# Layer norm and partial sums between attention and the feed-forward stage of a one-core encoder layer: where sums, scales and quarter sums are computed and in which order

## The chip, the core and the metric

The kernel runs on one core of a Trainium2 chip. The metric is the device time of one launch in microseconds (us), the median of several runs. Engines are named as in the profile: PE (matrix products), DVE, ACT and POOL (element-wise work), SP (which here only issues transfers).

## The reference

One transformer-like layer over 1056 tokens (1024 prompt tokens and 32 of a running stream) of width 1024. What matters here is the part after the mixers, with `x` the residual stream and `mix` the concatenated convolution and attention outputs times `w_o`:

```python
x = _layernorm(ALPHA * x + mix, ln1_g, ln1_b)     # mean, centred square mean, rsqrt, times g plus b
hid = relu(x @ w_ff1)                             # 1024 -> 4096
ff = (hid * hid) @ w_ff2                          # 4096 -> 1024
x = _layernorm(ALPHA * x + ff, ln2_g, ln2_b)
```

## The kernel before, in words

All activations stand transposed: features on the 128 partitions, tokens along the free axis. The 1024 features are eight row tiles, held in pairs: `z[i]` is 128 x 2 x 1056 in float32, and tile j is `z[j // 2][:, j % 2]`. Products are made to float32 precision from three half products: each operand is split into a rounded part `hi` and a rest `lo` (`split`, lines 106 to 111: `hi` on ACT in line 108, `lo` by a subtraction in line 111 on POOL or DVE), and `dense` (lines 127 to 133) issues hi*hi, hi*lo and lo*hi for each row tile k, in that order, on PE.

Tokens are cut three ways. CHUNKS are three blocks of 384, 384 and 288 tokens for the output projection and the first layer norm (chunk 0 is the last to be done). QUARTERS are four blocks of 264 tokens, counted from the end, so that quarter 3 and most of quarter 2 lie in or touch chunk 0. Halves of 528 tokens, together with halves of the features, give four blocks "11", "12", "21", "22", from which the fast matrix product of the feed-forward stage (seven products in place of eight) forms sums "t1" to "t4".

Between attention and feed-forward stands a list of short jobs, MID (lines 53 to 54), worked through in order (lines 832 to 834) by `job` (lines 692 to 713). A job's name is a kind, a chunk or quarter number and an index:
- `w0d`: output projection of attention for tile d of chunk 0 (`w_o_attn`, line 640 adds the product from PSUM to z on DVE).
- `lc0`, `lc1`, `lc2`: layer norm of chunk c: `ln_mean` (line 649: three DVE or POOL additions of tile pairs into one, line 652: PE products with a matrix of 1/1024, which leave the mean on every partition), `ln_var` (line 660: subtract the mean on DVE; lines 662 and 665: squares on ACT; line 666: three additions; line 669: PE products), `ln_scale` (line 674: square root on ACT; line 675: reciprocal on DVE; line 678: eight DVE instructions, z times g times 1/sigma). Chunk 2 adds on POOL, chunks 1 and 0 on DVE.
- `xc0`: `x1_out`: for each of the eight tiles ACT writes `hi` of z + b (line 784) and z + b itself (line 785), DVE (odd tiles) or POOL (even tiles) the rest `lo` (line 788); then z goes to memory in four transfers (line 790) on SP's queue.
- `fqe`: quarter q of four feature blocks e (CLASSIC) that are done by the ordinary product: 24 PE products of 264 columns, then a relu on ACT (line 798) and a product on DVE (line 799), which frees the PSUM bank, and a transfer out. Quarters 0 and 1 need chunks 2 and 1; quarters 2 and 3 need chunk 0, after `x00`.
- `tt`: `combine_x1` (lines 804 to 830): eight 1056-column subtractions on DVE (lines 823, 825, 826, 828) for the quarter sums, and eight splits of them (`split_sum`, lines 815 to 818: `hi` on ACT, `lo` on DVE or POOL). "t4" takes the place of block "12", which the jobs `f0e` and `f1e` read.

PSUM banks of this stage come from a pool of six ("mm2", lines 731 and 760) and one for the norms ("st_b", line 507). In this part a planner (the tile framework's simulated schedule) puts the instructions in order: the program's order is the priority, and the planner's cost estimates decide which instruction is put into an engine's queue next. On the chip each queue then runs strictly in that order.

After MID comes the feed-forward loop (`ff1_steps`, lines 870 to 953) in an order written out by hand: steps of 24 PE products (lines 856 to 858) with `run` (lines 1144 to 1157), which issues each step's loads and weight splits some steps ahead. The first seven steps use blocks 11, 21, t2, t1, t3, 22, t4 in that order; the second step adds onto the PSUM bank of the first, which ACT must have read before (line 906).

Of the kernel before, what the change touches and what calls it, by code (L numbers as in the profile page):

```python
# [15 lines left out]
OP = mybir.AluOpType  # L16
# [33 lines left out]
    (1, ("w13", "w14", "", "")),  # L50
    (0, ("", "w15", "w16", "w17")),
)
MID = tuple("w00 w01 w02 x20 w03 w04 l10 l11 l12 x10 w05 w06 w07 l00 f00 f10 f01 l01 f11 l02 x00 tt "
            "f20 f30 f21 f31 f02 f12 f22 f32 f03 f13 f23 f33".split())


def native(t, g2, i0):
# [12 lines left out]
def hybrid_layer(ctx, tc, xT, win, wkw, wo, w1, w2, ckT, cv, ckiT, scT, cw, lnp, rb, cst, oh,  # L70
# [574 lines left out]
    def ln_mean(c0, n, add_eng):  # L645
# [6 lines left out]
            PE.matmul(mean[:, :n], ones, s1[:, a], start=(a == 0), stop=(a == 1))  # L652
        return mean

    def ln_var(c0, n, add_eng, mean):
        cols = slice(c0, c0 + n)
        s2 = wide("junka", n)
        for i in range(4):
            zi = z[i][:, :, cols]
            V.tensor_tensor(zi, zi, mean[:, None, :n].to_broadcast([128, 2, n]), op=OP.subtract)  # L660
            if i == 0:
                S.activation(s2, zi, AF.Square)
            else:
                sq = wide("tie" if i % 2 else "rank", n)
                S.activation(sq, zi, AF.Square)
                add_eng.tensor_tensor(s2, s2, sq, op=OP.add)
        var = st_ps()
        for a in range(2):
            PE.matmul(var[:, :n], ones, s2[:, a], start=(a == 0), stop=(a == 1))
        return var  # L670

    def ln_scale(c0, n, which, var):
        rstd = scr.tile([128, 384], F32, name="rstd")
        S.activation(rstd[:, :n], var[:, :n], AF.Sqrt, bias=eps)
        V.reciprocal(rstd[:, :n], rstd[:, :n])
        for j in range(8):
            zj = z[j // 2][:, j % 2, c0:c0 + n]
            V.scalar_tensor_tensor(zj, zj, lnw[:, 2 * which, j:j + 1], rstd[:, :n], op0=OP.mult, op1=OP.mult)

    def ln(c0, n, which, add_eng):  # L680

        mean = ln_mean(c0, n, add_eng)
        ln_scale(c0, n, which, ln_var(c0, n, add_eng, mean))

    def conv_job(d):
        w = load_w(wo[d][:, 0:512], 4, 128)
# [5 lines left out]
    def job(name):  # L692
        if name == "tt":
            return combine_x1()
        kind, c, d = name[0], int(name[1]), int(name[2])
        if kind == "c":
            conv_job(d)
        elif kind == "w":
            w_o_attn(d, *CHUNKS[c], w=w_first[d] if c == 0 and d < 3 else None)
        elif kind == "t":  # L700
            topk((d,), True)
        elif kind == "x":
            x1_out(*CHUNKS[c])
        elif kind == "f":
            if d not in first:
                first[d] = load_w(w1[CLASSIC[d]], 8, 128)
            ff1(d, first[d], QUARTERS[c])
        elif d == 0:
            st[c] = ln_mean(*CHUNKS[c], (G if c == 2 else V))
        elif d == 1:  # L710
            st[c] = ln_var(*CHUNKS[c], (G if c == 2 else V), st[c])
        else:
            ln_scale(*CHUNKS[c], 0, st[c])

    for t, jobs in PLAN:
        for g2 in range(4):
# [61 lines left out]
    def x1_out(c0, n):  # L778
        cut = min(max(H - c0, 0), n)
        for j in range(8):  # L780
            zj, b = z[j // 2][:, j % 2, c0:c0 + n], lnw[:, 1, j:j + 1]
            spans = [(o, w) for o, w in ((0, cut), (cut, n - cut)) if w]
            for o, w in spans:
                S.activation(x1_part(j, c0 + o, w)[0], zj[:, o:o + w], AF.Identity, bias=b)
            S.activation(zj, zj, AF.Identity, bias=b)
            for o, w in spans:
                hi, lo = x1_part(j, c0 + o, w)
                (V if j % 2 else G).tensor_tensor(lo, zj[:, o:o + w], f32(hi), op=OP.subtract)
        for i in range(4):
            nc.sync.dma_start(zd[2 * i:2 * i + 2, :, c0:c0 + n].rearrange("j p t -> p j t"), z[i][:, :, c0:c0 + n])  # L790
# [13 lines left out]
    def combine_x1():  # L804
# [10 lines left out]
        def split_sum(name, i, raw, eng):  # L815
            hi = xf[name][:, 0, 2 * i:2 * i + 2]
            S.activation(hi, raw, AF.Copy)
            eng.tensor_tensor(xf[name][:, 1, 2 * i:2 * i + 2], raw, f32(hi), op=OP.subtract)

        for i in range(2):  # L820
            b11, b12 = z[i][:, :, :H], z[i][:, :, H:]
            b21, b22 = z[2 + i][:, :, :H], z[2 + i][:, :, H:]
            V.tensor_tensor(b11, b12, b11, op=OP.subtract)
            split_sum("t1", i, b11, V)
            V.tensor_tensor(b12, b22, b12, op=OP.subtract)
            V.tensor_tensor(b22, b22, b11, op=OP.subtract)
            split_sum("t2", i, b22, V)
            V.tensor_tensor(b21, b21, b22, op=OP.subtract)
            split_sum("t3", i, b12, G)
            split_sum("t4", i, b21, G)  # L830

    first = {}
    for name in MID:
# [310 lines left out]
    def run(steps, ahead, ahead_load):  # L1144

        n, prepared = len(steps), 0
        for i in range(-ahead_load, n):
            if i + ahead_load < n:
                for f in steps[i + ahead_load].load:
                    f()  # L1150
            while prepared < min(n, i + ahead + 1 if i > 0 else min(2, i + ahead + 1)):
                for f in steps[prepared].prep:
                    f()
                prepared += 1
            if i >= 0:
                for f in steps[i].mm + steps[i].post:
                    f()
# [293 lines left out]
```

## Time and profile before

| | us |
|---|---|
| median of 3 runs | 1326.07 (1323.88 to 1326.92) |
| the profiled execution, its own time | 1326.95 |
| its span, first to last instruction | 1325.2 |
| PE busy in the span | 1237.5 (93%) |
| DVE, ACT, POOL busy | 976.5, 692.7, 565.5 |

PE is nearly always busy; what can be gained is where it is not, or where its granted clock is low. "Busy" of PE is the union of pipelined instructions whose ends are modelled, so the pitch from start to start is the better price of one product. Times in the rows are us from the start of the span unless marked ns.

### The profile page before, as it was taken

What the parts mean: (1) busy time and instruction counts of PE and PEld (TensorE: products, weight loads), DVE (VectorE), ACT (ScalarE), POOL (GpSimd) and SP (SyncE); (2) the same over time, 40 slices, a digit from 0 to 9 for tenths busy, and PEclk for the clock granted to TensorE, in tenths of its full rate; (3) what the DMA queues carried; (4) which work ended last, traced back from release to release, by engine and by line L of the source; (5) the groups of instructions that cost most, each with busy time, mean ns of one, the idle gap of its engine ahead of it and who ended that gap; (6) DMA issues with size and microseconds to landing.
All of it is one profiled execution on the core that took longest, in us unless ns stands there. A gap on an engine that the chain in (4) does not pass through costs nothing. (4 is left out here: it accounts for less than half of the span.)

```text
span 1325.2 us, 24062 instructions
## 1 busy us (share of the span) xinstructions
PE 1237.5 (93%) x8822; PEld 1199.8 (91%) x8822; DVE 976.5 (74%) x2023; ACT 692.7 (52%) x1378; POOL 565.5 (43%) x452
## 2 busy tenths in 40 slices
PE   7999999998899989787899999999999999998894
PEld 6999999988898978676899999999999999998884
DVE  5675899999478888698466766767567567587766
ACT  5666988743798897765322222222434444443323
POOL 2412444523521342363444355444444444447632
PEclk9999999998999998897999999999999999999987
DMA  6321111135621221242134444344953653642201
GB/s 205 98 71 37 33 49 48 49 122 165 165 68 27 57 64 34 64 160 99 60 121 154 155 138 154 127 150 157 336 190 97 212 180 107 186 139 81 66 34 66
DMA packets 97221, 149.98 MB, mean 113 GB/s; under 512 B 12456, under 2 KB 41808, under 8 KB 97104
## 3 DMA queue, kind: packets, MB, share of 16 engines
q1 hardware_dynamic: 81664, 139.55, 32.4%
q0 software_dynamic: 9504, 4.33, 1.9%
q10 hardware_dynamic: 5936, 4.58, 1.2%
q8 instruction: 69, 1.13, 0.4%
q14 instruction: 48, 0.39, 0.1%
HBM read 105.41 MB, written 43.00 MB: 112 GB/s over the span
## 5 line engine op out<-in xcount | busy, mean ns | idle before, releaser
L111 POOL TENSOR_TENSOR whl<-wraw,whl 128x512 fp32r<-128x512 f32 (+1 forms) x184 | 251.7, 1373 | 413.1 <-ACT whl L108 394.1
L856 PE MATMUL acc<-b,whl 128*128 128x264 f32 x1088 | 310.9, 286 | 5.8 <-DVE ring L935 2.7
L857 PE MATMUL acc<-b,whl 128*128 128x264 f32 x1088 | 310.7, 286 | 0.0
L858 PE MATMUL acc<-b,whl 128*128 128x264 f32 x1088 | 309.2, 284 | 0.0
L856 PEld LDWEIGHTS acc<-b,whl 128*128 128x128 f32 x1088 | 205.5, 189 | 6.8 <-DVE ring L935 2.9
L108 ACT ACTIVATE whl<-wraw 128x512 fp32r<-128x512 f32 (+1 forms) x184 | 113.2, 623 | 178.8 <-DVE wraw L851 152.2
L858 PEld LDWEIGHTS acc<-b,whl 128*128 128x128 f32 x1088 | 206.0, 189 | 0.0
L857 PEld LDWEIGHTS acc<-b,whl 128*128 128x128 f32 x1088 | 205.1, 188 | 0.1
L132 PE MATMUL mm<-area,whl 128*128 128x384 f32 (+4 forms) x552 | 180.6, 328 | 0.4 <-DVE area L111 0.4
L131 PE MATMUL mm<-xh,whl 128*128 128x384 f32 (+4 forms) x520 | 170.2, 329 | 9.7 <-ACT whl L108 5.5
L133 PE MATMUL mm<-xh,whl 128*128 128x384 f32 (+4 forms) x520 | 169.0, 329 | 0.5 <-POOL whl L111 0.5
L111 DVE TENSOR_TENSOR b<-xraw,b 128x528 fp32r<-128x528 f32 x94 | 69.8, 742 | 86.4 <-ACT b L108 86.2
L108 ACT ACTIVATE b<-xraw 128x528 fp32r<-128x528 f32 x94 | 60.5, 644 | 135.5 <-PE acc L858 79.9
L441 ACT ACTIVATE junka<-s,cand 128x1024 bf16<-128x1024 f32 (+1 forms) x93 | 96.3, 1036 | 31.3 <-DVE cand L454 25.9
L131 PEld LDWEIGHTS mm<-xh,whl 128*128 128x128 f32 (+1 forms) x520 | 97.0, 187 | 12.5 <-ACT whl L108 6.2
L132 PEld LDWEIGHTS mm<-area,whl 128*128 128x128 f32 (+1 forms) x552 | 103.3, 187 | 3.2 <-DVE area L111 1.2
L133 PEld LDWEIGHTS mm<-xh,whl 128*128 128x128 f32 (+1 forms) x520 | 96.8, 187 | 4.0 <-POOL whl L111 1.4
L111 POOL TENSOR_TENSOR whl<-at,whl 128x512 fp32r<-128x512 f32 x56 | 81.0, 1457 | 30.7 <-ACT whl L108 30.7
L443 DVE TENSOR_SCALAR_CACHE_REDUCE junk<-s,cand 128x384 bf16<-128x384 f32 (+1 forms) x124 | 80.2, 647 | 1.1
L856 PE MATMUL acc<-area,whl 128*128 128x264 f32 x240 | 69.0, 287 | 0.0
L858 PE MATMUL acc<-area,whl 128*128 128x264 f32 x240 | 68.7, 286 | 0.0
L857 PE MATMUL acc<-area,whl 128*128 128x264 f32 x240 | 68.6, 286 | 0.0
(309 smaller groups left out, 3326.0 us busy)
## 6 DMA issues: line engine op xcount, KB each, us to landing
hd<-ring SPq DMA_DIRECT2D x98, 264.0 KB, 2.1
xraw<-hd SPq DMA_DIRECT2D x98, 264.0 KB, 2.7
at<-in_w_dram SPq DMA_DIRECT2D x58, 256.0 KB, 3.6
wraw<-in_win_dram SPq DMA_DIRECT2D x52, 256.0 KB, 2.6
wraw<-in_wo_dram SPq DMA_DIRECT2D x40, 256.0 KB, 2.7
w_a<-in_w_dram SPq DMA_DIRECT2D x23, 256.0 KB, 3.7
w_c<-in_w_dram SPq DMA_DIRECT2D x19, 256.0 KB, 3.2
zz<-zd SPq DMA_DIRECT2D x4, 1056.0 KB, 8.0
```

The costliest lines, as they stand in the source:

```text
L108: S.activation(hi, raw, AF.Copy)
L111: (lo_eng or G).tensor_tensor(lo, raw, f32(hi), op=OP.subtract)
L131: PE.matmul(ps, wh[k], a, start=(k == 0), stop=False)
L132: PE.matmul(ps, wh[k], b, start=False, stop=False)
L133: PE.matmul(ps, wl[k], a, start=False, stop=(k == K - 1))
L441: S.activation(junk(R, N), s, AF.Sign, bias=c, scale=-1.0, accum_out=cnt[:R, i:i + 1])
L443: V.tensor_scalar(junk(R, N), s, c, -float(k), op0=OP.is_ge, op1=OP.add, accum_out=cnt[:R, i:i + 1])
L856: PE.matmul(ps, wh, xhi, start=start, stop=False, skip_group_check=more)
L857: PE.matmul(ps, wh, xlo, start=False, stop=False, skip_group_check=more)
L858: PE.matmul(ps, wl, xhi, start=False, stop=stop, skip_group_check=more)
```

## The change

- Mean of chunk 0: the three additions and two PE products go; in their place PE multiplies each of the eight row tiles by the 1/1024 matrix, tile d - 1 after projection job d, all into one bank of the pool of six (`total`). Job `l00` then does nothing.
- Variance of chunk 0: the three additions go; each square goes into PE products by itself, eight in all (`ln_var_pe`). Chunks 1 and 2 keep their additions.
- Scale, all chunks: four DVE products of a tile pair with 1/sigma in place of eight with g and 1/sigma. g moves into `x1_out`, as the scale operand of the ACT instructions. For chunk 0 the float32 z is written by DVE (times g, plus b) and no longer by ACT.
- Quarter sums: the same eight subtractions and eight splits in the order t2, t1, t3, t4; both `lo` of t1 go from DVE to POOL, one each of t3 and t4 from POOL to DVE.
- MID: `f02` and `f12` come before `x00`, and `f03`, `f13` before `f22`.
- `run`: the preparation of the first feed-forward steps is no longer held to two.

```diff
--- before.py
+++ after.py
@@ -50,8 +50,8 @@
     (1, ("w13", "w14", "", "")),
     (0, ("", "w15", "w16", "w17")),
 )
-MID = tuple("w00 w01 w02 x20 w03 w04 l10 l11 l12 x10 w05 w06 w07 l00 f00 f10 f01 l01 f11 l02 x00 tt "
-            "f20 f30 f21 f31 f02 f12 f22 f32 f03 f13 f23 f33".split())
+MID = tuple("w00 w01 w02 x20 w03 w04 l10 l11 l12 x10 w05 w06 w07 l00 f00 f10 f01 l01 f11 f02 l02 f12 x00 tt "
+            "f20 f30 f21 f31 f03 f13 f22 f32 f23 f33".split())
 
 
 def native(t, g2, i0):
@@ -652,35 +652,42 @@
             PE.matmul(mean[:, :n], ones, s1[:, a], start=(a == 0), stop=(a == 1))
         return mean
 
+    def centred(c0, n, i, mean):
+
+        zi = z[i][:, :, c0:c0 + n]
+        V.tensor_tensor(zi, zi, mean[:, None, :n].to_broadcast([128, 2, n]), op=OP.subtract)
+        sq = wide(("junka", "tie", "rank", "tie")[i], n)
+        S.activation(sq, zi, AF.Square)
+        return sq
+
     def ln_var(c0, n, add_eng, mean):
-        cols = slice(c0, c0 + n)
-        s2 = wide("junka", n)
-        for i in range(4):
-            zi = z[i][:, :, cols]
-            V.tensor_tensor(zi, zi, mean[:, None, :n].to_broadcast([128, 2, n]), op=OP.subtract)
-            if i == 0:
-                S.activation(s2, zi, AF.Square)
-            else:
-                sq = wide("tie" if i % 2 else "rank", n)
-                S.activation(sq, zi, AF.Square)
-                add_eng.tensor_tensor(s2, s2, sq, op=OP.add)
+        s2 = centred(c0, n, 0, mean)
+        for i in range(1, 4):
+            add_eng.tensor_tensor(s2, s2, centred(c0, n, i, mean), op=OP.add)
         var = st_ps()
         for a in range(2):
             PE.matmul(var[:, :n], ones, s2[:, a], start=(a == 0), stop=(a == 1))
         return var
 
-    def ln_scale(c0, n, which, var):
+    def total(ps, d, a):
+
+        PE.matmul(ps, ones, a, start=(d == 0), stop=(d == 7))
+
+    def ln_var_pe(c0, n, mean):
+        var = st_ps()
+        for i in range(4):
+            sq = centred(c0, n, i, mean)
+            for a in range(2):
+                total(var[:, :n], 2 * i + a, sq[:, a])
+        return var
+
+    def ln_scale(c0, n, var):
         rstd = scr.tile([128, 384], F32, name="rstd")
         S.activation(rstd[:, :n], var[:, :n], AF.Sqrt, bias=eps)
         V.reciprocal(rstd[:, :n], rstd[:, :n])
-        for j in range(8):
-            zj = z[j // 2][:, j % 2, c0:c0 + n]
-            V.scalar_tensor_tensor(zj, zj, lnw[:, 2 * which, j:j + 1], rstd[:, :n], op0=OP.mult, op1=OP.mult)
-
-    def ln(c0, n, which, add_eng):
-
-        mean = ln_mean(c0, n, add_eng)
-        ln_scale(c0, n, which, ln_var(c0, n, add_eng, mean))
+        for i in range(4):
+            zi = z[i][:, :, c0:c0 + n]
+            V.tensor_tensor(zi, zi, rstd[:, None, :n].to_broadcast([128, 2, n]), op=OP.mult)
 
     def conv_job(d):
         w = load_w(wo[d][:, 0:512], 4, 128)
@@ -697,6 +704,11 @@
             conv_job(d)
         elif kind == "w":
             w_o_attn(d, *CHUNKS[c], w=w_first[d] if c == 0 and d < 3 else None)
+            if c == 0:
+                if d == 0:
+                    st[0] = mm_ps()
+                for e in ((d - 1, 7) if d == 7 else (d - 1,) if d else ()):
+                    total(st[0][:, :CHUNKS[0][1]], e, z[e // 2][:, e % 2, :CHUNKS[0][1]])
         elif kind == "t":
             topk((d,), True)
         elif kind == "x":
@@ -706,11 +718,12 @@
                 first[d] = load_w(w1[CLASSIC[d]], 8, 128)
             ff1(d, first[d], QUARTERS[c])
         elif d == 0:
-            st[c] = ln_mean(*CHUNKS[c], (G if c == 2 else V))
+            if c:
+                st[c] = ln_mean(*CHUNKS[c], (G if c == 2 else V))
         elif d == 1:
-            st[c] = ln_var(*CHUNKS[c], (G if c == 2 else V), st[c])
+            st[c] = ln_var(*CHUNKS[c], (G if c == 2 else V), st[c]) if c else ln_var_pe(*CHUNKS[0], st[0])
         else:
-            ln_scale(*CHUNKS[c], 0, st[c])
+            ln_scale(*CHUNKS[c], st[c])
 
     for t, jobs in PLAN:
         for g2 in range(4):
@@ -778,11 +791,14 @@
     def x1_out(c0, n):
         cut = min(max(H - c0, 0), n)
         for j in range(8):
-            zj, b = z[j // 2][:, j % 2, c0:c0 + n], lnw[:, 1, j:j + 1]
+            zj, g, b = z[j // 2][:, j % 2, c0:c0 + n], lnw[:, 0, j:j + 1], lnw[:, 1, j:j + 1]
             spans = [(o, w) for o, w in ((0, cut), (cut, n - cut)) if w]
             for o, w in spans:
-                S.activation(x1_part(j, c0 + o, w)[0], zj[:, o:o + w], AF.Identity, bias=b)
-            S.activation(zj, zj, AF.Identity, bias=b)
+                S.activation(x1_part(j, c0 + o, w)[0], zj[:, o:o + w], AF.Identity, scale=g, bias=b)
+            if c0:
+                S.activation(zj, zj, AF.Identity, scale=g, bias=b)
+            else:
+                V.tensor_scalar(zj, zj, g, b, op0=OP.mult, op1=OP.add)
             for o, w in spans:
                 hi, lo = x1_part(j, c0 + o, w)
                 (V if j % 2 else G).tensor_tensor(lo, zj[:, o:o + w], f32(hi), op=OP.subtract)
@@ -817,17 +833,20 @@
             S.activation(hi, raw, AF.Copy)
             eng.tensor_tensor(xf[name][:, 1, 2 * i:2 * i + 2], raw, f32(hi), op=OP.subtract)
 
+        b11, b12 = [z[i][:, :, :H] for i in range(2)], [z[i][:, :, H:] for i in range(2)]
+        b21, b22 = [z[2 + i][:, :, :H] for i in range(2)], [z[2 + i][:, :, H:] for i in range(2)]
         for i in range(2):
-            b11, b12 = z[i][:, :, :H], z[i][:, :, H:]
-            b21, b22 = z[2 + i][:, :, :H], z[2 + i][:, :, H:]
-            V.tensor_tensor(b11, b12, b11, op=OP.subtract)
-            split_sum("t1", i, b11, V)
-            V.tensor_tensor(b12, b22, b12, op=OP.subtract)
-            V.tensor_tensor(b22, b22, b11, op=OP.subtract)
-            split_sum("t2", i, b22, V)
-            V.tensor_tensor(b21, b21, b22, op=OP.subtract)
-            split_sum("t3", i, b12, G)
-            split_sum("t4", i, b21, G)
+            V.tensor_tensor(b11[i], b12[i], b11[i], op=OP.subtract)
+            V.tensor_tensor(b12[i], b22[i], b12[i], op=OP.subtract)
+            V.tensor_tensor(b22[i], b22[i], b11[i], op=OP.subtract)
+            split_sum("t2", i, b22[i], V)
+        for i in range(2):
+            split_sum("t1", i, b11[i], G)
+        for i in range(2):
+            split_sum("t3", i, b12[i], V if i else G)
+        for i in range(2):
+            V.tensor_tensor(b21[i], b21[i], b22[i], op=OP.subtract)
+            split_sum("t4", i, b21[i], V if i else G)
 
     first = {}
     for name in MID:
@@ -1148,7 +1167,7 @@
             if i + ahead_load < n:
                 for f in steps[i + ahead_load].load:
                     f()
-            while prepared < min(n, i + ahead + 1 if i > 0 else min(2, i + ahead + 1)):
+            while prepared < min(n, i + ahead + 1):
                 for f in steps[prepared].prep:
                     f()
                 prepared += 1
```

## Rows read from the trace of the kernel before

**Rows 1.** Windows, all engines: busy us (instructions), PE clock, DMA share, GB/s.
```profile
558.00:576.00 18.00, 18.00 (x102) 17.70 (x102) 12.79 (x14) 14.59 (x32) 12.63 (x12) 0.97 0.50 154
...
593.60:598.00 4.40, 0.07 (x2) 0.07 (x1) 4.22 (x7) 2.15 (x5) 0.00 (x0) 0.86 0.22 76
598.00:605.40 7.40, 2.86 (x4) 1.11 (x4) 3.85 (x4) 1.23 (x3) 0.00 (x0) 0.50 0.03 9
605.40:610.40 5.00, 4.98 (x22) 4.98 (x23) 5.00 (x7) 5.00 (x11) 2.25 (x2) 0.50 0.24 84
610.40:619.80 9.40, 9.40 (x78) 9.24 (x76) 8.65 (x7) 5.18 (x9) 5.93 (x4) 1.00 0.79 264
...
624.10:633.20 9.10, 6.44 (x42) 6.23 (x40) 9.10 (x8) 5.62 (x11) 6.97 (x4) 0.81 0.00 0
```

**Rows 2.** PE timeline, 584 to 653: start, duration, instruction, [idle before <-releaser].
```profile
584.28 1.56 PE L652 MATMUL st_b<-junk,cs 128*128 128x384 f32 x4
...
585.38 0.58 PE L131 MATMUL mm<-b,whl 128*128 128x264 f32 x1
...
597.96 2.90 PE L669 MATMUL st_b<-junka,cs 128*128 128x384 f32 x4 [4.33 <-DVE junka L666]
...
605.42 1.47 PE L131 MATMUL mm<-b,whl 128*128 128x264 f32 x5 [4.56 <-ACT b L784]
...
623.12 0.39 PE L132 MATMUL mm<-b,whl 128*128 128x264 f32 x1 [3.27 <-DVE b L788]
...
633.17 0.39 PE L131 MATMUL mm<-b,whl 128*128 128x264 f32 x1 [2.66 <-DVE xraw L799]
...
652.31 0.29 PE L856 MATMUL acc<-b,whl 128*128 128x264 f32 x1
```

**Rows 3.** DVE timeline, 579 to 640, same columns.
```profile
579.63 1.45 DVE L649 TENSOR_TENSOR junk<-z,z 128x768 f32<-128x768 f32 x1
...
581.94 2.29 DVE L649 TENSOR_TENSOR junk<-junk,z 128x768 f32<-128x768 f32 x2
...
584.15 6.25 DVE L788 TENSOR_TENSOR b<-z,b 128x144 fp32r<-128x144 f32 x6
...
590.66 3.53 DVE L660 TENSOR_TENSOR z<-z,st_b 128x768 f32<-128x768 f32 x4
...
601.51 2.55 DVE L675 RECIPROCAL rstd<-rstd 128x384 f32<-128x384 f32 x1 [3.70 <-ACT rstd L674]
...
604.10 5.08 DVE L678 SCALAR_TENSOR_TENSOR z<-z,lnw,rstd 128x384 f32<-128x384 f32 x8
...
620.28 2.32 DVE L818 TENSOR_TENSOR area<-z,area 128x1056 fp32r<-128x1056 f32 x1
...
622.52 0.55 DVE L788 TENSOR_TENSOR b<-z,b 128x384 fp32r<-128x384 f32 x1
...
638.91 1.25 DVE L818 TENSOR_TENSOR area<-z,area 128x1056 fp32r<-128x1056 f32 x1
```

**Rows 4.** Groups of DVE by line, 470 to 660: count | busy us, mean ns.
```profile
L678 DVE SCALAR_TENSOR_TENSOR z<-z,lnw,rstd 128x384 f32<-128x384 f32 x16 | 12.2, 828 | 0.0
...
L666 DVE TENSOR_TENSOR junka<-junka,tie 128x768 f32<-128x768 f32 x4 | 3.8, 946 | 0.0
```

**Rows 5.** Waits, 557 to 600: engine, line, released by: total us, times, longest.
```profile
PE mm L132 <- DVE b L788: 2.8, 4, 1.2
```

**Rows 6.** Groups of DVE by line, 360 to 420, same columns as rows 4.
```profile
L491 DVE TENSOR_SCALAR s<-s,cand 128x384 f32<-128x384 f32 x2 | 0.8, 404 | 0.0
```

**Rows 7.** Groups of ACT by line, 470 to 660.
```profile
L785 ACT ACTIVATE z<-z,lnw 128x384 f32<-128x384 f32 x16 | 9.2, 602 | 0.0
```

**Rows 8.** Groups of POOL by line, 540 to 660.
```profile
L818 POOL TENSOR_TENSOR bt<-z,bt 128x1056 fp32r<-128x1056 f32 x4 | 11.3, 2840 | 13.7 <-ACT bt L817 13.7
```

**Rows 9.** POOL timeline, 619 to 652, columns as in rows 2.
```profile
619.19 2.29 POOL L111 TENSOR_TENSOR whl<-wraw,whl 128x512 fp32r<-128x512 f32 x1
...
646.44 4.91 POOL L818 TENSOR_TENSOR bt<-z,bt 128x1056 fp32r<-128x1056 f32 x2 [11.36 <-ACT bt L817]
```

## The prediction, made before the changed kernel ran

> **What bounds the kernel now.** I looked first at the windows around the change, then at PE's timeline in them for its gaps, then at DVE's, because the gaps name it. Before 558 us and after 652 us PE has work at hand; between them it has not. In the windows [rows 1] PE is full from 558 to 576 (the output projection of chunk 0), almost idle from 593.6 to 598, and from 598 to 605.4 does four slow products only. The PE timeline [rows 2] says what ended the gaps: 4.33 us until DVE had added the squares (L666), 4.56 us until the first tile of x1 of chunk 0 was there, 3.27 us for one late `lo` on DVE (L788), 2.66 us for a PSUM bank that DVE had not emptied (L799): 14.8 us in all. The waits before 600 [rows 5] add 2.8 us, again for `lo` on DVE. The granted clock is 0.50, the lower of the two levels, in the two windows behind the first gap, and 0.81 from 624.1 to 633.2 [rows 1]. What it costs: 78 products in 9.40 us are 0.12 us each at 1.00; 22 in 5.00 us are 0.23 us at 0.50 [rows 1]. So in this stage the limit is the chain through chunk 0's norm, and DVE's queue behind it: DVE is busy for at least 92% of each window from 593.6 to 633.2 but the one of the root, 598 to 605.4. The stage ends when the feed-forward loop begins on PE, at 652.3 [rows 2].
>
> **The ceiling.** From 558.0 to 652.3 is 94.3 us. Needed are 18.0 us for the projection [rows 1], 16 `f` jobs x 24 products x 0.12 = 46.3 us, and the products of the norm. Four of those took 1.10 us from their first start to the next start of other work, 584.28 to 585.38 [rows 2]; one call in the program is two such instructions, so a call costs 0.55 us. Before there are four calls in the stage, 2.2 us. That leaves 27.8 us of gaps and slow clock. After the change there are 16 calls, 8.8 us, and PE needs 18.0 + 46.3 + 8.8 = 73.1 us: it could be done at 631.1, 21.2 us earlier. No gain can be larger, unless outside this stage.
>
> **Part by part.**
>
> *Sums to PE.* Three additions for the mean leave DVE: 1.45 + 2.29 = 3.74 us [rows 3]. Three for the variance leave: 3 x 0.946 = 2.84 us [rows 4]. They cost PE 12 more calls: 6.6 us at 0.55; at the lower clock four instructions took 2.90 us [rows 2], 1.45 us a call, so 17.4 us is the other end. I take 0.55, since most come while PE has `f` jobs between them. The mean's first seven can run as soon as each tile is added to z; only the last waits for tile 7.
>
> *Scale in pairs.* For chunk 0 eight took 5.08 us [rows 3], so of 12.2 us for both big chunks [rows 4] chunk 1 had 7.1. No row shows four products of z with 1/sigma. Nearest is a 768-column sum of two SBUF tiles, 0.946 us [rows 4]: four are 3.8 us. Gains: 1.3 us in chunk 0, 3.3 in chunk 1. If the pairs meet POOL as chunk 1's singles did, up to 7.1 us: no gain. I take 3.8. Chunk 2's saving lies in attention, where I count nothing (it can only shorten DVE).
>
> *g into x1_out.* The scale operand of ACT: the instruction stays one per tile over the same columns, so I keep its 0.602 us [rows 7]; no row has it with this operand, and a tenth of that either way, 0.06 us a tile, is 0.5 us over eight. Chunk 0's float32 z moves from ACT (8 x 0.602 = 4.8 us [rows 7]) to DVE. The nearest DVE row with two operations on 384 columns is 0.404 us [rows 6]: 3.2 us; far end 0.828 [rows 4], 6.6 us. The `lo` of a tile now waits for DVE's own queue instead of ACT's. SP's transfers of z wait for DVE likewise, and the feed-forward weights stand behind them in SP's queue; as the z is needed by nobody soon and the first weights only 30 us later, nothing.
>
> *Chain of chunk 0.* Before, the subtraction of the mean began at 590.66, though the mean's products had begun at 584.28: six `lo` of chunk 1 took 6.25 us between [rows 3]. With 3.74 + 3.3 us less in DVE's queue it begins at 583.7 at best, 587 if only the additions help; I take 585. From there: 3.5 us of subtraction [rows 3], the last square 0.8 us (768 columns in one instruction, so between the 0.602 of 384 columns [rows 7] and twice that), its two calls 1.1, root 0.65 (600.86 to 601.51 [rows 2, 3]), reciprocal 2.55, first pair 0.95, its `hi` 0.6: 595.2 us. Before it was 605.4. Half of that comes from DVE's shorter queue, half from the additions leaving the chain.
>
> *f02 and f12 before x00.* 48 products, 5.8 us, which fall where PE stood. PE's own queue is then: 558.0 + 18.0 + 4.4 (mean) + 6 x 2.9 (`f`) + 4.4 (variance) = 602.2 us. This is later than 595.2, so chunk 0's chain ends before PE comes to need it, with 7 us to spare. That is the point of the forecast: both long gaps close, and with them the reason for most of the slow clock. `lo` of chunk 0 follow from the reciprocal's end at 593.6: + 3.8 + 3.2 + 4 x 0.55 [rows 3] = 602.8 us: just in time.
>
> *Quarter sums and `run`.* The same eight subtractions and eight splits: no work goes. t2 and t1 are used 5.8 and 8.7 us after the loop begins; POOL needs 2 x 2.84 us for t1 [rows 8], with some 30 us to do it. The cover is the `f` jobs: without it, 5.7 us. The late `lo` at 622.52 [rows 3] stood behind these sums in DVE's queue, 3.27 us of PE; the earlier chain makes that less likely, but the planner may repeat it. Preparing four steps, not two: nothing, up to 1.2 us of ACT (two splits of 0.6) either way.
>
> *What stays.* Mean in the pool of six: one bank less for `w` and `f` from 558 to about 588, price between 0 and the 5 us that DVE can be away on scales and `lo`. I leave: `lo` of chunk 1, 2 of the 2.8 us; waits for a bank, 2.7 as now; `lo` of chunk 0, 1.0; slow clock, 1.5 (of 22 products at 0.11 more, 2.4). Together 7.2 us. 631.1 + 7.2 = 638.3 against 652.3: **14.0 us less**. The profiled execution took 1326.95 us for a span of 1325.2, 0.9 above the median of 1326.07; from the median the forecast is 1312.
>
> **A rule against it.** DVE's same split instruction took 2.32 us at 620.28 and 1.25 us at 638.91 [rows 3], the first while POOL worked (from 619.19 for 2.29 us), the second in POOL's idle 11.36 us before 646.44 [rows 9]. The Trainium skill (SBUF — State Buffer, section SBUF: two separate sides) has DVE instructions with two SBUF inputs and POOL block each other for a whole instruction. The trace agrees with it in these two rows. By that rule moving t1 to POOL relieves nothing, as the two take turns, and the time would be that of rival A, not that of the sum above.
>
> **Rivals.**
>
> A. *DVE and POOL hold each other up.* After the reciprocal DVE has about 3.8 + 3.2 + 2.2 + 12 x 1.25 (sums, splits) = 24 us of work, and POOL at least 4 x 2.84 and the weights' `lo`. If each 1.25 becomes the 2.32 seen [rows 3], DVE has 12.8 us more, and banks and `lo` come late: I give PE half of it, 6.4 us. Gain 8 us, 1318. For: DVE was full until 633 [rows 1]. Against: six DVE additions fewer, and six banks of slack. The rule above is a form of this rival.
>
> B. *The filling does not happen.* The planner puts `f02`, `f12` later, or no bank is free because the mean holds one, so the edit does not do what it says. Then PE waits for the chain to 595 to 598 and f2x run at the lower clock at first; 5.8 us of cover are lost, with 2 to 4 us of clock: gain 4 to 6 us, 1321. For: in the trace before, PE did not take these jobs in the gap. Against: their place in the program was after x00.
>
> C. *Slower: PE's queue stands at the new calls.* Each waits, in order, for one DVE addition or one ACT square, and the `f` jobs behind it wait too. If the 12 added calls run at the lower clock on the path they cost 17.4 us; the shorter chain gives back 10.2, `f02` and `f12` fill nothing. Net +7: 1333. It decides when the wait per call passes about 0.9 us over all twelve. Against: the mean's calls follow tiles done one job earlier.
>
> **How the numbers follow.** Forecast 0.62, A 0.22, B 0.09, C 0.07. Predicted 1312 us. The range starts at 1305, the ceiling's 21.2 us, since each of the four waits left in may vanish, and ends at 1321: A is in, and the better half of B; the rest of B and C are out. About 0.2% (2.7 us) is what a measurement of this kernel can tell from no change. Faster by more: forecast, A and most of B, 0.89; same: rest of B and the best of C, 0.05; slower: 0.06.
>
> **What would show it.** Right: no PE gap over 2 us between 576 and 605; `f02` and `f12` on PE before the first product of quarter 2; subtraction of the mean beginning near 585; clock near 1.00 there; the first product of the feed-forward loop (L856 before) near 638. Scale pairs near 0.95 us and the new DVE z near 0.4 us show the prices. Wrong: a gap at the `total` line released by DVE or ACT, a late subtraction of the mean, `lo` of chunk 0 behind the quarter sums again, or a feed-forward step that waits for t1 or t2.

## The result, and the profile after

The changed kernel took 1319.88 us (median of 12 runs, 1315.28 to 1324.26), the kernel before 1326.59 us in runs of the same sitting: ratio 0.9944, 95% interval 0.9930 to 0.9958. It is 6.7 us faster by the medians and 7.4 by the ratio; the forecast had 14.0, rival A 8. One of the 12 executions of the kernel before took 3066.67 us, which moves its median by 0.3 us. The profiled execution took 1320.45 us for a span of 1318.6.

"The stage" below is from PE's first product of `w00` to the first of the feed-forward loop: 557.85 to 652.31, 94.5 us before [rows 2]; 555.07 to 645.38, 90.3 us after. So the two traces differ by 4.2 us inside the stage and by 2.8 ahead of it. The whole stage as one window (columns as in [rows 1]), before and then after:

```profile
557.85:652.31 94.46, 76.31 (x490) 71.79 (x489) 74.49 (x82) 51.05 (x100) 48.50 (x35) 0.88 0.33 110
```
```profile
555.07:645.38 90.31, 79.69 (x514) 73.78 (x513) 70.83 (x76) 52.45 (x94) 60.65 (x37) 0.94 0.33 108
```

PE's idle time in it went from 18.15 us to 10.62, 7.5 less; its busy time went from 76.31 to 79.69, 3.4 more. Ahead of the stage, the first difference is a wait of DVE on a transfer of `tie`. Its row in the kernel before, then after:

```profile
353.08 0.55 DVE L414 SCALAR_TENSOR_TENSOR z<-tie,mm_b 128x384 f32<-128x384 f32 x1 [2.04 <-DMA tie<-in_xT_dram]
```
```profile
351.26 0.55 DVE L414 SCALAR_TENSOR_TENSOR z<-tie,mm_b 128x384 f32<-128x384 f32 x1 [0.41 <-DMA tie<-in_xT_dram]
```

It stands ahead of every changed instruction (the first is at 492.8), and in `after_old_sums`, which has most of the change, it begins at 353.20. So this 1.8 us belongs to single executions and not to the change. In the 12 traces of whole kernels behind this document the stage begins between 552.18 and 557.26 with chunk 2's scale in pairs and between 555.51 and 557.85 without; one trace of each kernel can't say how much of the 2.8 us is the change's. The stage itself, after, in windows of all engines (columns as in [rows 1]), and the page's busy times:

```profile
593.60:598.00 4.40, 4.40 (x32) 3.87 (x31) 0.37 (x1) 0.82 (x2) 0.00 (x0) 1.00 0.00 0
598.00:605.40 7.40, 6.05 (x50) 5.83 (x48) 7.40 (x10) 4.57 (x10) 0.65 (x1) 1.00 0.09 23
605.40:610.40 5.00, 4.35 (x22) 4.04 (x23) 5.00 (x10) 1.15 (x2) 3.25 (x4) 0.67 0.97 322
610.40:619.80 9.40, 3.35 (x23) 3.15 (x22) 7.38 (x9) 2.17 (x2) 9.40 (x2) 0.86 0.47 162
619.80:624.10 4.30, 4.30 (x21) 4.30 (x21) 2.17 (x2) 2.88 (x6) 4.30 (x3) 0.50 0.09 31
624.10:633.20 9.10, 9.10 (x76) 9.10 (x75) 9.10 (x7) 5.19 (x8) 9.10 (x5) 0.99 0.10 32
...
PE 1238.0 (94%) x8846; PEld 1198.8 (91%) x8846; DVE 972.9 (74%) x2013; ACT 692.4 (53%) x1370; POOL 574.2 (44%) x452
```

In the two holes of [rows 1] PE is now busy for all of 593.6 to 598 and for 6.05 of the 7.40 us from 598 to 605.4, at clock 1.00, as forecast. A new hole stands at 610.4 to 619.8, where PE had 78 products before and has 23 now, and behind it the clock is at 0.50, the lower level. PE's timeline after, with all its waits over 0.5 us in the stage, some of its calls for the norm, and the end of the stage:

```profile
573.94 0.91 PE L674 MATMUL mm<-z,cs 128*128 128x384 f32 x2 [2.57 <-DVE z L640]
574.39 0.63 PE L131 MATMUL mm<-area,whl 128*128 128x384 f32 x1
574.86 0.34 PE L132 MATMUL mm<-area,whl 128*128 128x384 f32 x1
...
589.48 1.45 PE L674 MATMUL st_b<-junka,cs 128*128 128x384 f32 x4
590.77 1.45 PE L674 MATMUL st_b<-tie,cs 128*128 128x384 f32 x4
592.06 1.45 PE L674 MATMUL st_b<-rank,cs 128*128 128x384 f32 x4
593.05 0.58 PE L131 MATMUL mm<-b,whl 128*128 128x264 f32 x1
...
595.53 1.45 PE L674 MATMUL st_b<-tie,cs 128*128 128x384 f32 x4
...
605.97 0.39 PE L132 MATMUL mm<-b,whl 128*128 128x264 f32 x1 [1.92 <-POOL b L804]
...
618.69 0.59 PE L132 MATMUL mm<-b,whl 128*128 128x264 f32 x1 [6.04 <-POOL b L804]
...
645.38 0.29 PE L875 MATMUL acc<-b,whl 128*128 128x264 f32 x1
```

Three waits, 10.5 us. The largest is for the last even `lo` of chunk 0, tile 6, on POOL (line 804, before line 788). POOL's timeline, then DVE's:

```profile
607.69 1.25 POOL L804 TENSOR_TENSOR b<-z,b 128x384 fp32r<-128x384 f32 x1 [0.29 <-DVE z L801]
610.09 8.54 POOL L804 TENSOR_TENSOR b<-z,b 128x384 fp32r<-128x384 f32 x1 [1.16 <-DVE z L801]
```
```profile
565.98 7.44 DVE L690 TENSOR_TENSOR z<-z,rstd 128x768 f32<-128x768 f32 x4
573.34 0.55 DVE L640 TENSOR_TENSOR z<-mm,z 128x384 f32<-128x384 f32 x1
...
585.34 3.53 DVE L658 TENSOR_TENSOR z<-z,mm 128x768 f32<-128x768 f32 x4
...
597.63 2.55 DVE L687 RECIPROCAL rstd<-rstd 128x384 f32<-128x384 f32 x1 [7.10 <-ACT rstd L686]
...
600.39 3.55 DVE L690 TENSOR_TENSOR z<-z,rstd 128x768 f32<-128x768 f32 x4
...
610.79 1.25 DVE L839 TENSOR_TENSOR z<-z 128x1056 f32<-128x1056 f32 x1
...
616.53 1.25 DVE L841 TENSOR_TENSOR z<-z,z 128x1056 f32<-128x1056 f32 x1
621.93 0.43 DVE L815 TENSOR_TENSOR xraw<-mm,xraw 128x264 f32<-128x264 f32 x1 [4.15 <-ACT xraw L814]
```

The same instruction takes POOL 1.25 us at 607.69 and 8.54 at 610.09. DVE meanwhile runs `lo`, quarter sums and a sum of weights without a pause until 617.78, and POOL ends at 618.63, 0.85 us after that: it got its turn when DVE had nothing left. DVE had the subtraction of the mean at 585.34 (forecast 585), but the reciprocal began at 597.63, where the forecast has about 591. ACT's timeline says why:

```profile
587.59 0.83 ACT L660 ACTIVATE tie<-z 128x768 f32<-128x768 f32 x1
588.32 0.83 ACT L660 ACTIVATE rank<-z 128x768 f32<-128x768 f32 x1
...
592.31 0.84 ACT L660 ACTIVATE tie<-z 128x768 f32<-128x768 f32 x1 [2.24 <-PE st_b L674]
597.02 0.58 ACT L686 ACTIVATE rstd<-st_b,eps 128x384 f32<-128x384 f32 x1 [3.87 <-PE st_b L674]
```

The fourth square goes into the buffer of the second, `tie`, which PE has to read first. PE reads it late, since its products stand in the queue behind `f` jobs, and the products of the fourth, at 595.53, stand behind another job.

### The profile page after: what moved, and what is told of

Read it like the earlier page. It is cut to its first block, busy times and chain, and to the rows that moved or that the text cites. A ratio compares the mean times of both kernels' runs of the same rounds, so it can differ in the third digit from the quotient of the medians.

```text
span 1318.6 us, 24093 instructions
## 1 busy us (share of the span) xinstructions
PE 1238.0 (94%) x8846; PEld 1198.8 (91%) x8846; DVE 972.9 (74%) x2013; ACT 692.4 (53%) x1370; POOL 574.2 (44%) x452
## 5 line engine op out<-in xcount | busy, mean ns | idle before, releaser
L131 PE MATMUL mm<-xh,whl 128*128 128x384 f32 (+4 forms) x520 | 170.1, 328 | 10.2 <-ACT whl L108 5.5
```

The source lines that it names most:

```text
L131: PE.matmul(ps, wh[k], a, start=(k == 0), stop=False)
```

## Experiments

The runs share one question: what took back half of the 14 us. The suspects are POOL held up by DVE, the longer chain of the variance, and work that the change adds to full engines. Ratios are to the kernel before, on the same chip, with 95% intervals; the table gathers them with the stage of each profiled execution, which is one execution per kernel.

| run | ratio | stage, us |
|---|---|---|
| the change | 0.9944 (0.9930 to 0.9958) | 90.3 |
| lo6_dve | 0.9930 (0.9914 to 0.9947) | 88.3 |
| after_old_mid | 0.9971 (0.9956 to 0.9986) | 91.5 |
| after_old_quarters | 0.9946 (0.9916 to 0.9976) | 93.0 |
| after_old_sums | 0.9967 (0.9950 to 0.9984) | 89.4 |
| before_new_mid | 0.9926 (0.9908 to 0.9944) | 86.2 |
| tt_late | 0.9925 (0.9908 to 0.9941) | 89.6 |
| before_pe_sums_mid | 0.9951 (0.9935 to 0.9968) | 89.2 |
| after_z_act | 0.9974 (0.9964 to 0.9985) | 93.9 |
| four_squares | 0.9938 (0.9922 to 0.9954) | 88.0 |
| best | 0.9926 (0.9913 to 0.9940) | 86.6 |

**POOL's late `lo` goes to DVE** (changed kernel, one instruction moved):

```diff
-                (V if j % 2 else G).tensor_tensor(lo, zj[:, o:o + w], f32(hi), op=OP.subtract)
+                (V if j % 2 or (c0 == 0 and j == 6) else G).tensor_tensor(lo, zj[:, o:o + w], f32(hi), op=OP.subtract)
```

> The changed kernel with one instruction moved: the rest (lo) of tile 6 of chunk 0 is subtracted on DVE, not POOL. Theory 1 (POOL is locked out while DVE runs instructions with two SBUF sources without a pause): the 8.54 us subtraction on POOL goes, DVE takes about 0.55 us for it, PE's wait of 6.04 us and the stretch at the lower clock behind it go; 1310 to 1315 us, a ratio to before near 0.990. Theory 2 (DVE's queue is the bound, and PE only waits elsewhere for banks or later lo): 1318 to 1322 us, ratio 0.994 to 0.996, with a new PE wait of 4 us or more released by DVE.

1316.43 us. The wait of 6.04 is gone, but POOL's next instruction, the first split of t1, now waits out the same run of DVE, and PE waits for a `lo` of weights queued behind it (POOL's timeline, then PE's):

```profile
613.35 7.35 POOL L834 TENSOR_TENSOR area<-z,area 128x1056 fp32r<-128x1056 f32 x1 [4.30 <-ACT area L833]
620.66 1.25 POOL L111 TENSOR_TENSOR whl<-wraw,whl 128x512 fp32r<-128x512 f32 x1
```
```profile
621.97 0.39 PE L133 MATMUL mm<-b,whl 128*128 128x264 f32 x1 [2.33 <-POOL whl L111]
...
629.51 0.39 PE L133 MATMUL mm<-b,whl 128*128 128x264 f32 x1 [1.78 <-POOL whl L111]
```

The stage is 2.0 us shorter, 0.75 of it at the wait for the mean near 573; most of the 6 us moved to the next instruction on POOL. The two intervals overlap.

**Does POOL wait out a run of DVE by itself?** The changed kernel with a measurement behind its last instruction, hence its long total: POOL subtracts 128x384 alone, then beside ten DVE instructions of 1056 columns with two SBUF inputs, with one, and beside forty that read PSUM.

```diff
+        G.tensor_tensor(pl[:, :384], rg[0][:, :384], pl[:, :384], op=OP.subtract)
...
+            for k in range(10):
+                d = rg[1 + k if k < 2 else 3 + k % 4]
+                if k == 1:
+                    G.tensor_tensor(pl[:, :384], rg[1][:, :384], pl[:, :384], op=OP.subtract)
+                if kind == 0:
+                    V.tensor_tensor(d, rg[0], d, op=OP.subtract)
+                elif kind == 1:
+                    V.tensor_scalar(d, d, 0.5, 0.5, op0=OP.mult, op1=OP.add)
...
```

> The changed kernel, and behind its last instruction a measurement: POOL subtracts two 128x384 tiles alone, then while DVE runs ten 1056-column instructions without a pause, with two SBUF sources, with one SBUF source and two constants, and with one source in PSUM. Theory 1: about 1 us alone; with two SBUF sources until DVE's run ends, 8 us or more; about 1 us with the PSUM source; the one-source case either way. Theory 2 (the 8.54 us came from something else in the kernel): 1 to 2.5 us in all four.

POOL's timeline behind the kernel's end:

```profile
1318.94 0.99 POOL L1398 TENSOR_TENSOR mb<-mb,mb 128x384 f32<-128x384 f32 x1 [13.50 <-DVE mb L1395]
1321.58 1.88 POOL L1404 TENSOR_TENSOR mb<-mb,mb 128x384 f32<-128x384 f32 x1 [1.65 <-DVE mb L1406]
1333.72 1.32 POOL L1404 TENSOR_TENSOR mb<-mb,mb 128x384 f32<-128x384 f32 x1 [10.26 <-DVE mb L1408]
1340.97 0.99 POOL L1404 TENSOR_TENSOR mb<-mb,mb 128x384 f32<-128x384 f32 x1 [5.93 <-DVE mb L1411]
```

0.99 alone, 1.88 beside the two-input form, 1.32 beside the one-input form, 0.99 beside PSUM readers. So the two do exclude each other, but here POOL got in behind a single instruction. By itself a run of DVE doesn't lock POOL out to its end; the 8.54 us isn't explained by this.

**The same with other operands**: contiguous rows, halves as in the quarter sums without and with each reading the last one's result, and the last with one PSUM reader among them.

```diff
...
+        def halves_chain(k):
+            d = rg[1][:, :, k % 2 * H:k % 2 * H + H]
+            V.tensor_tensor(d, rg[1][:, :, (k + 1) % 2 * H:(k + 1) % 2 * H + H], d, op=OP.subtract)
...
```

> The changed kernel with a second measurement behind its end: a 128x384 subtraction on POOL that arrives in a run of eight two-source DVE instructions: contiguous, in halves of 528 without dependence, in halves each waiting for the last, and the latter with one PSUM-source instruction in fifth place. If the form of the DVE instructions decides: some of the four take 6 us or more, and the fourth under 6. If POOL always gets in behind one DVE instruction, as in the first measurement: 1.5 to 2.5 us in all, and the long ones in the kernel have another cause.

1.80, 1.88, 1.88 and 1.88 us: the form doesn't decide. What releases POOL inside the kernel stays open.

**The old order of jobs**, all else as changed:

```diff
-MID = tuple("w00 w01 w02 x20 w03 w04 l10 l11 l12 x10 w05 w06 w07 l00 f00 f10 f01 l01 f11 f02 l02 f12 x00 tt "
-            "f20 f30 f21 f31 f03 f13 f22 f32 f23 f33".split())
+MID = tuple("w00 w01 w02 x20 w03 w04 l10 l11 l12 x10 w05 w06 w07 l00 f00 f10 f01 l01 f11 l02 x00 tt "
+            "f20 f30 f21 f31 f02 f12 f22 f32 f03 f13 f23 f33".split())
```

> The changed kernel with the old order of the job list: f02, f12 behind x00, f03 and f13 late. Theory 1 (these jobs fill the wait for chunk 0's norm and nothing else would): PE has a gap of 4 us or more before chunk 0's first product, and the time goes up by 4 to 8 us against the changed kernel, 1324 to 1328. Theory 2 (what counts is when tile 6's lo comes, so PE's work can lie before or behind it): within 2 us of the changed kernel, 1318 to 1322.

1322.62 us, 3.6 us more than the changed kernel by the ratios, a little less than the 4 to 8 expected; the other parts of the change without the new order still give 0.9971. PE waits 4.41 us for the first `hi` of chunk 0 again, as [rows 2] has it with 4.56. POOL's `lo` of tile 6 took 2.81 us: DVE came to an instruction that reads PSUM at 611.21, and POOL was done 0.94 us after that.

```profile
609.34 2.81 POOL L804 TENSOR_TENSOR b<-z,b 128x384 fp32r<-128x384 f32 x1 [1.16 <-DVE z L801]
```

**The old quarter sums**, all else as changed: the loop of the diff's last part as it was before.

```diff
...
-            split_sum("t1", i, b11[i], G)
...
+            split_sum("t1", i, b11, V)
...
```

> The changed kernel with the quarter sums in the old order and on the old engines. Theory 1: DVE then splits t1 right behind its first subtraction and waits for ACT between, so POOL gets in: tile 6's lo takes under 4 us and the time is 1313 to 1318. Theory 2 (the order doesn't matter, DVE's sum of work does): 1318 to 1322.

1319.70 us, the changed kernel's time by the median, though POOL's `lo` took 10.88 us beside a longer run of DVE (to 618.70) and PE waited 8.37 for it; under 4 us was expected.

```profile
608.67 10.88 POOL L804 TENSOR_TENSOR b<-z,b 128x384 fp32r<-128x384 f32 x1 [1.16 <-DVE z L801]
```

Moving t1 to POOL bought nothing that this comparison can tell. But the median hides a spread: of the 12 runs four took 1309.95 to 1311.66 us, five 1318.64 to 1321.76 and three 1325.75 to 1328.24. The trace is of the middle group. The four are below every run of any other kernel here (the lowest is 1313.97), and what is different in them no trace shows.

**The old sums of chunk 0 on DVE**, all else as changed:

```diff
...
-            st[c] = ln_var(*CHUNKS[c], (G if c == 2 else V), st[c]) if c else ln_var_pe(*CHUNKS[0], st[0])
+            st[c] = ln_var(*CHUNKS[c], (G if c == 2 else V), st[c])
```

(and `l00`'s mean likewise, without the calls in the `w0` jobs)

> The changed kernel with the mean and the variance of chunk 0 summed on DVE as before (six additions, four PE calls). If the PE products earn by shortening DVE's queue and the chain: 4 to 8 us more than the changed kernel, 1323 to 1328, the mean's subtraction 4 us or more later than 585. Rival (with f02 and f12 as cover the chain is hidden, and PE saves 6.6 us of calls): 1316 to 1320.

1322.60 us: by the ratios 3.0 us more than the changed kernel, with intervals that overlap a little; 4 to 8 was expected. POOL's `lo` took 8.54 us again, so this wait doesn't come with the sums on PE. PE waits for the mean on DVE (2.48 us) and for the first `hi` (2.71), but is busy for 74.69 us of the stage in place of 79.69.

**The new order of jobs alone**: the kernel before with the new MID line and nothing else.

> The kernel before with the new order of the job list alone. If the order earns by itself: f02 and f12 cover the wait at 593.6 to 605.4, 5 to 8 us less than before, ratio 0.994 to 0.996. Rival (DVE's late lo and late banks take it back without the other parts): within 2 us of before, ratio 0.9985 to 1.0015.

1317.26 us, 0.9926: this one line gives as much as the whole change, and by the middle of the intervals (which overlap) 2.4 us more. PE's timeline, and the stage as one window:

```profile
602.49 0.75 PE L131 MATMUL mm<-b,whl 128*128 128x264 f32 x4 [3.62 <-ACT b L784]
604.82 0.59 PE L132 MATMUL mm<-b,whl 128*128 128x264 f32 x1 [1.57 <-POOL b L788]
...
620.29 0.59 PE L132 MATMUL mm<-b,whl 128*128 128x264 f32 x1 [3.08 <-DVE b L788]
...
642.16 0.29 PE L856 MATMUL acc<-b,whl 128*128 128x264 f32 x1
```
```profile
555.97:642.16 86.19, 74.25 (x491) 70.60 (x490) 75.56 (x82) 50.61 (x100) 48.77 (x35) 0.92 0.36 120
```

PE is idle for 11.94 us, 1.3 more than in the changed kernel, and busy for 5.4 us less, without the 12 added calls.

Its subtraction of the mean begins at 588.78, 3.4 us later than in the changed kernel, and its reciprocal at 598.43, only 0.8 later: 9.7 us from one to the other, where the changed kernel has 12.3.

**The new order and the sums on PE**, on the kernel before:

> The kernel before with the new job order and the PE sums for chunk 0; scale, x1_out, quarter sums and run as before. The new job order alone had given a ratio of 0.9926. If the PE sums shorten the chain: 2 to 5 us below that, ratio 0.988 to 0.991. Rival (they lengthen it again, since the last square waits for a buffer that PE still reads, and its products stand behind other products in PE's queue): ratio 0.992 to 0.995.

1319.55 us, 0.9951: the sums on PE make the kernel with the new order no faster, and by the middle of the intervals (which overlap a little) 3.3 us slower. Subtraction at 584.86 and reciprocal at 597.92, against 588.78 and 598.43: of 3.9 us at the chain's head 0.5 is left at its end. ACT's timeline shows the same wait for `tie` as in the changed kernel:

```profile
592.60 0.84 ACT L660 ACTIVATE tie<-z 128x768 f32<-128x768 f32 x1 [2.24 <-PE st_b L674]
```

**A buffer of its own for the fourth square**, on the changed kernel:

```diff
-        sq = wide(("junka", "tie", "rank", "tie")[i], n)
+        sq = wide(("junka", "tie", "rank", "tie" if c0 else "junk")[i], n)
```

> The changed kernel with a buffer of its own for the fourth square of chunk 0 (junk, free there since the additions went) in place of the second's. If the wait for that buffer sets the root: the fourth square starts before 590 rather than at 592.3, the reciprocal 1.5 to 3 us sooner than at 597.6, and the time goes down by 0 to 3 us, since POOL's late lo follows behind. Rival (the last products stand behind block products in PE's queue anyway): the reciprocal within 0.7 us of where it was.

1317.96 us. The fourth square follows the third at once (591.52), and subtraction to reciprocal is 10.4 us in place of 12.3. But the planner put more `lo` of chunk 1 ahead of the subtraction (587.80), so the reciprocal came at 598.21, no earlier; the stage, too, began 1.2 us later in this trace. POOL's four `lo` took at most 1.65 us each, PE's wait for them is gone, and a wait for a PSUM bank that DVE empties took its place:

```profile
627.49 0.59 PE L131 MATMUL mm<-b,whl 128*128 128x264 f32 x1 [4.55 <-DVE xraw L815]
```

**Quarter sums later** (`lo6_dve` with `tt` behind `f31`):

```diff
-MID = tuple("w00 w01 w02 x20 w03 w04 l10 l11 l12 x10 w05 w06 w07 l00 f00 f10 f01 l01 f11 f02 l02 f12 x00 tt "
-            "f20 f30 f21 f31 f03 f13 f22 f32 f23 f33".split())
+MID = tuple("w00 w01 w02 x20 w03 w04 l10 l11 l12 x10 w05 w06 w07 l00 f00 f10 f01 l01 f11 f02 l02 f12 x00 f20 f30 f21 f31 tt f03 f13 f22 f32 f23 f33".split())
```

> The changed kernel with tile 6's lo on DVE and the quarter sums (tt) behind f31 in the job list, no longer ahead of f20. Theory 3 (DVE's run of sums, put ahead of everything that PE waits for, is the cost; taking one lo off POOL only moved the wait to the weights of block 3): PE waits released by POOL between 600 and 640 fall from 6 us to under 2 us and the time is 1308 to 1313 us, a ratio of 0.986 to 0.991. Rival (DVE and POOL have too much work before the loop's third product, wherever it stands): PE waits as long for t2, t1 or banks; 1315 to 1320, ratio 0.993 to 0.996.

1317.57 us, where 1308 to 1313 was expected. PE's waits for POOL fall to 1.92 us; at 627.00 it waits 4.72 for a bank, since DVE does the quarter sums there.

**Chunk 0's float32 z back on ACT**, all else as changed:

```diff
-            if c0:
-                S.activation(zj, zj, AF.Identity, scale=g, bias=b)
-            else:
-                V.tensor_scalar(zj, zj, g, b, op0=OP.mult, op1=OP.add)
+            S.activation(zj, zj, AF.Identity, scale=g, bias=b)
```

> The changed kernel with chunk 0's float32 z written by ACT as for the other chunks. If the eight DVE instructions for z are what makes DVE's run without a pause and lets POOL wait for 8.54 us: that subtraction takes under 4 us, PE's wait of 6.04 us goes, 1312 to 1316, ratio 0.989 to 0.992. Rival (ACT then is as late as DVE was, with 16 instructions of 0.69 us): 1317 to 1321.

1321.86 us, not the 1312 to 1316 expected. POOL's longest `lo` is 1.82 us, but PE waits for DVE instead: three late `lo` (5.3 us) and a bank (4.77 us at 631.52).

**What should be best of these**: the kernel before with the sums on PE, four buffers for the squares, the new order and `tt` behind `f31`; scale, parameters and quarter sums as before.

> The kernel before with the PE sums (a buffer for each square) and the new job order with the quarter sums behind f31; scale, x1_out and the quarter sums' own order as before. If the late lo of tile 7 and the sums ahead of it were the last large wait of the job order alone (3.1 us and the slow clock behind it): 1308 to 1313, ratio 0.985 to 0.990. Rival (DVE's and POOL's work has to be done before the loop's third product wherever it stands): ratio 0.991 to 0.995.

1316.15 us, 0.9926; the hoped-for 1308 to 1313 didn't come. The reciprocal (595.27) is the earliest of all runs, and PE has no wait between 579 and 614.5. From the subtraction (584.39) it is still 10.9 us, where the forecast had about 6. Then PE waits 4.12 us for a late `lo` on DVE and 1.94 for a bank. The time lies 1.8 parts in a thousand below the changed kernel (the intervals overlap) and level with the new order alone.

## Why the prediction was right and wrong

**Right.** Faster, inside the range, near its upper end. The filling worked: `f02` and `f12` ran between the variance's products and in front of quarter 2, no PE wait stands between 576 and 604, and the clock is 1.00 there; `after_old_mid` brings the 4.4 us gap back. DVE was ready for the subtraction at 585.3 (585 forecast), and PE's queue was filled to 604.0 (602.2 forecast). `before_new_mid` shows that the order of the jobs pays by itself. The two parts don't add up: the rest of the change without it gives 0.9971 (`after_old_mid`), the order alone 0.9926, both together 0.9944. That the time lies in the range is in part luck: the stage, where all of the gain was forecast, shows 4.2 us, which from 1326.07 would be 1322, past the range's end; the rest of the measured gain came from outside it.

**Wrong: the size.** The forecast let 7.2 us stand over the 73.1 that PE needs. The stage has 90.3, so 17.2: PE idle for 10.6 us and busy for 79.7, where 5.7 and 74.6 were forecast. Three waits make 10.5, where 5.7 was allowed; of that, the 2.0 for `lo` of chunk 1 and the 2.7 for a bank didn't come at all. Products at the lower clock make about 4, where 1.5 was allowed: 24 from 618.69 to 624.1 took 5.4 us in place of 2.9, and some 15 from 607 to 610.5 took 0.22 us each in place of 0.12. The rest, by subtraction 2.7, lies mostly (some 1.8) in the 16 calls of the norm, each with the products beside it: 3.57 us for six calls of the variance is 0.60, and a call of the mean with the product behind it takes 0.45 + 0.47 us (573.94 to 574.86), where the product alone takes 0.17, so 0.75 (right behind a wait). I had 0.55.

By steps:

- *"`lo` of chunk 0 ... just in time", 1.0 us left.* This failed most: 1.92 + 6.04 us, and much of the slow clock behind them. It is rival A, that DVE and POOL hold each other up, in a sharper form than its price (each 1.25 us becomes 2.32): one short POOL instruction waited through eight of DVE's, which themselves took no longer (1.25 us for a quarter sum). The Trainium skill (SBUF — State Buffer, section SBUF: two separate sides) has the loser stand until the winner's instruction is done. The isolated measurement agrees (1.88 us, of which 0.99 is POOL's own), the kernel's 8.54 us goes beyond it, and the measurement decides.
- *The chain, "its two calls 1.1".* From subtraction to reciprocal I had about 6, it took 12.3, more than the 10.85 of the kernel before [rows 3] and the 9.7 of `before_new_mid`. The reciprocal ended at 600.18, 6.6 us behind the forecast's 593.6, and all `lo` of chunk 0 with it. I priced the products and left out the queue that they stand in: PE takes them in order among `f` jobs, and the buffer used twice ties ACT to PE's place in that queue. Moving the sums did free DVE, and gave nearly all of it back here. `before_pe_sums_mid` and `best` show what the buffer costs: nearly the same start, 13.1 and 10.9 us. The rest is the place in the queue.
- *Sums to PE, 6.6 us of PE time.* Priced about right, but I counted it beside a gain of 10.2 us in the chain that didn't come. In the traces it is a cost on a PE that the new order has filled: `before_new_mid`, without these calls, has the shortest stage of all runs, 86.2. By whole times the sign isn't shown: on the kernel before with the new order the sums on PE cost 3.3 us, in the changed kernel taking them off PE cost 3.0 (`after_old_sums`), and in both pairs the intervals overlap.
- *Scale in pairs, 3.3 us in chunk 1.* The far end came: 7.44 us for four, beside POOL, against 7.1 for eight singles; in chunk 0, 3.55 (3.8 forecast). A call of the mean stood in PE's queue behind the pairs by way of z (line 640) and cost 2.57 us, a wait that PE hadn't had between 558 and 576 [rows 1], and that is 0.70 us with the singles in `before_pe_sums_mid`. That is rival C at one call out of sixteen.
- *Scale operand in ACT, 0.06 us at most.* It was 0.09, as shown below; over sixteen instructions of chunk 0's `hi` and chunk 1's z some 1.5 us of ACT, which no wait of PE shows.
- *Quarter sums, no work goes.* `after_old_quarters` has the same median, with the spread told above. Nor did any feed-forward step wait for t1 or t2.

**What is shown and what isn't.** Shown: five kernels in which POOL's wait was removed or shortened, by five different edits, gained at most 2.5 us over the changed one by the ratios, and two of them lost; their traces have PE wait for something else in its place, mostly in the queues of DVE or POOL (weights, a bank, a late `lo` of DVE; in `after_old_mid` also the first `hi`). No kernel's ratio is below 0.9925. That these two engines between norm and loop are the joint limit once PE is filled is argued from those waits; the four runs of `after_old_quarters` near 1310 us are open under it. Not shown either: what the scale in pairs and the edit of `run` are worth, since no run takes back either alone. Nor is it shown why POOL waits for the end of DVE's run in the kernel. In the changed kernel, `after_old_quarters` and `lo6_dve` it ended 0.85, 0.85 and 2.4 us after DVE had paused or come to a PSUM reader, its own time or nearly that; two isolated measurements did not reproduce it. How much of the 2.8 us ahead of the stage lasts over many runs is open too, beyond the transfer shown at 353 us.

## What to carry to other kernels

Put independent work that is already there into the gap before shortening the chain that makes the gap: on the kernel before, one line of job order gave all of this gain by itself. A sum moved to an engine that takes its work in order costs its place in that engine's queue, and every buffer used twice ties the producer to that place. If the same change fills that engine, count the sum's time there as a cost too. Where DVE and POOL both have long two-input work, look at which small result stands beside the long run, and expect that freeing it uncovers the next one. Look at the single runs as well as at their median.

## What the runs showed of the hardware

- ACT with a scale operand from memory takes about 0.09 us more, at 144 columns as at 384. The groups of ACT from 470 to 660 us, after (before: 602 for 384 columns [rows 7]):

```profile
L799 ACT ACTIVATE z<-z,lnw 128x384 f32<-128x384 f32 x8 | 5.3, 694 | 0.0
L797 ACT ACTIVATE b<-z,lnw 128x144 fp32r<-128x144 f32 x8 | 4.0, 494 | 1.1 <-DVE z L690 1.1
```

  The 144-column form took 404 ns before. The Trainium skill (ScalarE: Activation LUTs, section What ACT_TABLE_LOAD costs) has each such operand add about 93 ns; the trace agrees, with 92 and 90.
- POOL's time beside DVE depended on what DVE reads: 0.99 us beside PSUM readers, 1.32 beside one SBUF input, 1.88 beside two, for the same 128x384 subtraction; inside the kernel one took up to 10.88.
- DVE's multiply and add with two per-partition operands on 384 columns, 0.404 us in its nearest row [rows 6], took a mean of 0.685 us in chunk 0, with POOL at its `lo` beside it.
